# Three orders changed in a one-core encoder layer: mixing's first splits, the opening of cross-attention, the end of the down projection

## The chip, the cores and the metric

The kernel runs on one core of one Trainium2 chip. The time is the device time of one execution in microseconds (us); lower is better. The core has five engines, each with an instruction queue of its own that is worked off in order: TensorE (PE: matmuls and transposes), VectorE (DVE), ScalarE (ACT), GpSimd (POOL) and SyncE (SP), which here issues nearly all DMAs. An instruction waits on semaphores until what it reads is written and what it overwrites has been read; everything behind it on its engine waits with it.

## The reference

One step of an encoder layer for 2048 prompt rows (16 tiles of 128) and 128 sample rows (one tile, 8 streams of 16), width 1024:

```python
def encoder_layer(x, ...):
    h = rmsnorm(x, g_mix_pre)
    y, new_k, new_v, new_conv = parallel_mixer(h, ...)   # band attention (8 heads) | depthwise conv, then @ w_out
    x = x + rmsnorm(y, g_mix_post)
    h = rmsnorm(x, g_mem_pre)
    x = x + rmsnorm(memory_attention(h, mk, mv, w_mq, w_mo), g_mem_post)   # 4 heads, 256 memory rows
    h = rmsnorm(x, g_ffn_pre)
    f = (silu(h @ w_gate) * (h @ w_up)) @ w_down                           # hidden width 2816
    return x + rmsnorm(f, g_ffn_post)
```

## The kernel before

Every large matmul is made in three: both operands are split into a high and a low part (`hi` in a rounded format, a cast on ScalarE; `lo = x - hi`, mostly on VectorE), and the products hi·hi, hi·lo and lo·hi are summed in PSUM (`mm3`, `mm3h`). So each operand tile costs one cast and one subtraction before TensorE can use it, and "split" below means these two.

The phases follow each other: memory projections; input projection and convolution; band attention; mixing (`mixout`); cross-attention (`cross_open` begins it, `phase_cross` goes on); gate and up projections (`gate_up`); `down`. A scheduling layer orders the instructions of each engine at build time by its own estimates and priorities. `issue_after(ins)` forces every instruction written inside it that runs on the engine of `ins` to stand behind `ins` there; instructions on other engines, DMAs among them, are not held. In the traces `sbf`, `sbr` and `sbx` are the large SBUF regions (plain numbers; split halves), `flexb` further SBUF pieces, `psb` PSUM.

Three places matter:

1. *Attention to mixing.* `attention()` walks over 128 units (head, tile): scores, softmax (`L802` reduces on VectorE, `L804` takes exponentials on ScalarE), transposes of the probabilities (`L883`, split by `L884` and `L885`), products with the values (`L896`, of which `L900` and `L902` gather the result). One sample stream goes along with each head; at its end two copies on VectorE (`L852`, `L853`) take its result from a PSUM buffer. `weigh` turns the softmax sums of one tile into factors: its transpose (`L970`) uses the same ring of three PSUM buffers. Meanwhile the output weights are loaded and split (`wload`: `L277`, `L278`); four of the eight remain for `mixout`. There `prep(t)` splits a tile's convolution half and its attention half (`L1024`, `L1025`), and the products with the output weights (`L291`) begin with the sample tile, then tile 0.
2. *Mixing to cross-attention.* `cross_open` is called inside the last mixed tile. It loads and splits the first cross weights `f1` (0 and 1 of 8) and norms tile 0: `prenorm` squares (`L308`), scales (`L315`), transposes (`L318`), casts the high half (`L319`) and subtracts the low one (`L320`). `phase_cross` loads `f1` 2 to 7 and the value weights `f2` (`L1218`, split in `L1221` and `L1222`; the subtractions of `f1` 1, 3 and 5 are on GpSimd) through three staging buffers `stg`. `scores` of tile 0 are 48 products, in whose midst `second()` norms tile 1; the scores of tile 1 follow, with `probs` of tile 0 (`L1280` to `L1284`) in between. The postnorm of the sample's cross-attention (`L339` to `L341`) and of the last mixed tiles (`L1071` to `L1077`) run at the same time.
3. *The end of `down`.* Seven weight forms are gone through in the order 0, 1, 3, 4, 5, 6, 2; each has three groups of tile pairs, a group three PSUM products of 11 blocks. The activation block is loaded (`L1596`) and split (`L1601`, `L1602`) once for the group's products. `evict` adds a product into `ys`; a tile that is complete is normed and stored by `finish` (`L351` squares, `L352` multiplies by the gain, `L300` and `L301` take the power, `L357` scales and adds the residual, loaded at `L1613` into one of two buffers). Form 2 completes tiles 12, 13 and the sample tile last; there `finish` works in two halves.

Of the kernel before, what the change touches and what calls it, by code (L numbers as in the profile page):

```python
# [8 lines left out]
F32 = mybir.dt.float32  # L9
# [3 lines left out]
ALU = mybir.AluOpType  # L13
# [4 lines left out]
P = 128  # L18
D = 1024
# [19 lines left out]
F2 = 2  # L39
SLAST = NPT * (H - 1) + 4  # L40
# [96 lines left out]
class Build:  # L137
# [173 lines left out]
    def prenorm(self, pool, pspool, xt, gbc, hi, lo, tag="tr", keep=False):  # L311
        nc = self.nc
        r = self.rms(pool, xt[:, :])
        h = self.t(pool, [P, D], F32, "hn", 1) if keep else xt
        nc.vector.scalar_tensor_tensor(h[:, :], xt[:, :], r[:, :], gbc[:, :], ALU.mult, ALU.mult)  # L315
        ps = self.t(pspool, [P, KC, P], F32, tag)
        for k in range(KC):
            self.last_transpose = nc.tensor.transpose(ps[:, k, :], h[:, k * P:(k + 1) * P], self.ident[:, :])  # L318
        nc.scalar.copy(hi, ps[:, :, :])  # L319
        nc.vector.tensor_tensor(lo, ps[:, :, :], hi.bitcast(F32), ALU.subtract)  # L320
# [22 lines left out]
    def finish(self, pool, y, xt, gbc, dst, parts, engine):  # L343
# [5 lines left out]
        yg = self.t(pool, [P, D], F32, "po")  # L349
# [442 lines left out]
    def attention(self):  # L792
# [14 lines left out]
        def sample(s):  # L807
# [45 lines left out]
            nc.vector.tensor_copy(self.attS[DH:, :, ss], po[DH:, :, DEC_S:])  # L853
# [135 lines left out]
    def mixout(self, ctx):  # L989
# [13 lines left out]
        for _ in self.wo_load:  # L1003
            pass
# [33 lines left out]
        with self.tc.high_priority(offset=HP2):  # L1038
            for t in order[:2]:
                prep(t)  # L1040
# [202 lines left out]
    def phase_cross(self, ctx):  # L1243
# [79 lines left out]
        todo = [(g, p) for g in range(3) for p in range(3)]  # L1323
        def second():
            hq[1] = norm(1)
# [5 lines left out]
        with self.tc.issue_after(self.last_mo.ins):  # L1331
# [181 lines left out]
    def down(self, ctx):  # L1513
# [12 lines left out]
                .at("y", 4, *[(a, [0]) for a in fy]))  # L1526
# [60 lines left out]
        for i, j in enumerate(order):  # L1587
            w = nxt
            nxt = []
            for g in range(3):  # L1590
                np_ = 3 if g < 2 or j in (0, 2, 4, 6) else 2
                ps = [self.t(ps_mm, [P, 512], F32, "mm") for _ in range(np_)]
                for f0 in range(0, NF // 2, 2):
# [3 lines left out]
                    for x in range(nf):  # L1597
# [5 lines left out]
                        fp = f0 + x  # L1603
                        for p in range(np_):
# [5 lines left out]
                for p in range(np_):  # L1610
                    for t in evict(j, g, p, ps[p]):
                        xt = self.t(pool, [P, D], F32, "xt")
                        nc.sync.dma_start(xt[:, :], self.x2[t])  # L1613
                        end = i == len(order) - 1 and g == 2
                        self.finish(pool, ys[t], xt, gpost, self.rows("y", t), 2 if end else 1,
                                    nc.vector if end else nc.gpsimd)
# [74 lines left out]
```

## Time and profile before

| | |
|---|---|
| time, median of 3 runs | 2942.23 us (2939.48 to 2942.48) |
| profiled execution | 2946.83 us, its span 2945.0 us |
| mean granted TensorE clock | 0.994 |
| DMA | 500.04 MB in 198154 packets, mean 170 GB/s |
| chain that ended last | PE 41%, DMA 4%, POOL 3%, DVE 2% of the span |

The span is counted from the first to the last instruction of the program on the chip. Rows of a timeline give start and length in us, engine, line, operation, what is written from what, sizes, a count of like instructions, and in brackets the idle time of the engine before it and what ended it. A "window" row gives, for a stretch of the span, the busy time of each engine with its count of instructions, the clock that TensorE was granted (1.00 is full), the share of the DMA engines and GB/s.

### The profile page before, as it was taken

What the parts mean: (1) busy time and instruction counts of PE and PEld (TensorE: products, weight loads), DVE (VectorE), ACT (ScalarE), POOL (GpSimd) and SP (SyncE); (2) the same over time, 40 slices, a digit from 0 to 9 for tenths busy, and PEclk for the clock granted to TensorE, in tenths of its full rate; (3) what the DMA queues carried; (4) which work ended last, traced back from release to release, by engine and by line L of the source; (5) the groups of instructions that cost most, each with busy time, mean ns of one, the idle gap of its engine ahead of it and who ended that gap; (6) DMA issues with size and microseconds to landing.
All of it is one profiled execution on the core that took longest, in us unless ns stands there. A gap on an engine that the chain in (4) does not pass through costs nothing.

```text
span 2945.0 us, 45369 instructions
## 1 busy us (share of the span) xinstructions
PE 2871.7 (98%) x16740; PEld 2623.9 (89%) x16740; DVE 2083.8 (71%) x3024; ACT 1308.8 (44%) x2661; POOL 1375.9 (47%) x1252
## 2 busy tenths in 40 slices
PE   8999999989999999999989999999999999999998
PEld 8999999979978777888879999999999999888786
DVE  6697795979985345344569788788788997556655
ACT  4535364669973234232344333433344444332433
POOL 0268396730023224144557565465556775424413
PEclk9999999999999999999999999999999999999999
DMA  8635255558845665133355333644344446756754
GB/s 306 248 115 174 97 162 172 161 173 202 214 141 193 214 228 179 57 127 102 129 196 176 115 133 115 201 161 156 135 148 143 149 141 224 224 172 227 226 192 163
DMA packets 198154, 500.04 MB, mean 170 GB/s; under 512 B 18981, under 2 KB 87085, under 8 KB 189603
## 3 DMA queue, kind: packets, MB, share of 16 engines
q1 hardware_dynamic: 187211, 459.78, 48.3%
q0 software_dynamic: 10720, 37.36, 3.3%
q8 instruction: 131, 2.15, 0.3%
q14 instruction: 92, 0.75, 0.1%
HBM read 365.97 MB, written 141.81 MB: 172 GB/s over the span
## 4 chain that ended last, share of the span: by engine, by line
PE 41%; DMA 4%; POOL 3%; DVE 2%; issue 1%; ACT 0%; DVEq 0%; SPq 0%; POOLq 0%; ACTq 0%
PE psb L285 13%; PE psb L283 13%; PE psb L284 13%; PE psb L291 1%; DMA sbf<-x 1%; DMA sbf<-in_w_down_dram 1%; POOL sbf L1541 1%; DMA sbf<-hn 1%; PE psb L1396 1%; DMA sbf<-in_w_gate_dram 0%; DVE sbr L1419 0%; POOL sbf L340 0%; DMA out_dram<-sbf 0%; DVE sbr L1602 0%; DMA hn<-sbf 0%
## 5 line engine op out<-in xcount | busy, mean ns | idle before, releaser
L283 PE MATMUL psb<-sbr 128*128 128x384 f32 (+3 forms) x2808 | 942.3, 337 | 4.4 <-ACT sbr L1601 1.9
L284 PE MATMUL psb<-sbr 128*128 128x384 f32 (+3 forms) x2356 | 805.3, 342 | 2.4 <-DVE sbr L320 2.4
L285 PE MATMUL psb<-sbr 128*128 128x512 f32 (+3 forms) x1848 | 633.1, 344 | 3.3 <-DVE sbr L1602 3.1
L283 PEld LDWEIGHTS psb<-sbr 128*128 128x128 f32 x2808 | 530.0, 189 | 34.4 <-ACT sbr L1601 3.4
L285 PE MATMUL psb<-sbr,sbx 128*128 128x384 f32 (+2 forms) x1484 | 476.4, 322 | 0.0
L284 PEld LDWEIGHTS psb<-sbr 128*128 128x128 f32 x2356 | 444.7, 189 | 29.4 <-DVE sbr L320 2.7
L285 PEld LDWEIGHTS psb<-sbr 128*128 128x128 f32 x1848 | 347.9, 189 | 33.3 <-DVE sbr L1602 6.6
L1419 DVE TENSOR_TENSOR sbr<-sbf,sbr 128x512 fp32r<-128x512 f32 x258 | 263.7, 1025 | 38.7 <-ACT sbr L1418 37.9
L1418 ACT CAST sbr<-sbf 128x512 fp32r<-128x512 f32 x258 | 159.4, 620 | 279.7 <-PE psb L284 223.6
L285 PEld LDWEIGHTS psb<-sbr,sbx 128*128 128x128 f32 x1484 | 280.3, 189 | 0.2
L523 DVE SCALAR_TENSOR_TENSOR psb<-sbf,psb 128x768 f32<-128x768 f32 (+1 forms) x290 | 264.3, 911 | 6.2
L291 PE MATMUL psb<-sbr 128*128 128x512 f32 x1004 | 247.3, 395 | 0.1
L1602 DVE TENSOR_TENSOR sbr<-sbf,sbr 128x384 fp32r<-128x384 f32 (+1 forms) x231 | 171.1, 763 | 94.6 <-ACT sbr L1601 93.7
L291 PEld LDWEIGHTS psb<-sbr 128*128 128x128 f32 x1004 | 185.9, 188 | 41.5 <-issue 2.5
L278 POOL TENSOR_TENSOR sbx<-sbf,sbr 128x1024 fp32r<-128x1024 f32 x60 | 153.1, 2553 | 81.6 <-ACT sbr L277 78.2
L1541 POOL TENSOR_TENSOR sbf<-sbf 128x512 f32<-128x512 f32 x77 | 107.5, 1401 | 169.7 <-DMA sbf<-in_w_down_dram 167.9
L1601 ACT CAST sbr<-sbf 128x384 fp32r<-128x384 f32 (+1 forms) x231 | 111.2, 497 | 166.5 <-PE psb L284 141.1
L533 POOL TENSOR_TENSOR flexb<-flexb,flexb 128x128 f32<-128x128 f32 (+1 forms) x180 | 167.5, 931 | 21.4 <-ACT flexb L532 12.0
L283 PE MATMUL psb<-sbr,sbx 128*128 128x384 f32 (+1 forms) x524 | 170.5, 327 | 2.2 <-ACT sbx L1418 1.5
L1418 ACT CAST sbx<-sbf 128x512 fp32r<-128x512 f32 x153 | 94.6, 620 | 162.2 <-PE psb L284 150.7
L291 PE MATMUL psb<-sbr,sbx 128*128 128x512 f32 x654 | 160.9, 397 | 3.7 <-ACT sbx L319 2.2
L1419 DVE TENSOR_TENSOR sbx<-sbf,sbx 128x512 fp32r<-128x512 f32 x153 | 152.3, 997 | 16.3 <-ACT sbx L1418 16.0
(333 smaller groups left out, 5938.4 us busy)
## 6 DMA issues: line engine op xcount, KB each, us to landing
af<-flexb SPq DMA_DIRECT2D x33, 1344.0 KB, 6.2
sbf<-in_w_down_dram SPq DMA_DIRECT2D x154, 256.0 KB, 3.7
sbf<-af SPq DMA_DIRECT2D x90, 384.0 KB, 4.0
sbf<-in_w_gate_dram SPq DMA_DIRECT2D x66, 512.0 KB, 3.4
sbf<-in_w_up_dram SPq DMA_DIRECT2D x66, 512.0 KB, 3.4
sbf<-x SPq DMA_DIRECT2D x50, 512.0 KB, 3.8
sbf<-in_w_in_dram SPq DMA_DIRECT2D x48, 512.0 KB, 3.7
sbr<-ks SPq DMA_DIRECT2D x28, 512.0 KB, 9.0
```

What stands on the lines that cost most here:

```text
L278: self.lo_engine.tensor_tensor(lo[:, :], wf[:, :], hi[:, :].bitcast(F32), ALU.subtract)
L283: nc.tensor.matmul(ps, lh, rh, start=start, stop=False, **kw)
L284: nc.tensor.matmul(ps, lh, rl, start=False, stop=False, **kw)
L285: self.last_product = nc.tensor.matmul(ps, ll, rh, start=False, stop=stop, **kw)
L291: self.last_half = nc.tensor.matmul(y[o], l, r[:, o * 512:(o + 1) * 512], start=start and x == 0, stop=stop and x == 2)
L523: nc.vector.scalar_tensor_tensor(acc if w < CW - 1 else o, src(w), cwt[:, j, w:w + 1], acc, ALU.mult, ALU.add)
L533: nc.gpsimd.tensor_tensor(o, o, v, ALU.add)
L1418: nc.scalar.copy(hs[j][:, :], src[j])
L1419: nc.vector.tensor_tensor(ls[j][:, :], src[j], hs[j][:, :].bitcast(F32), ALU.subtract)
L1541: nc.gpsimd.tensor_tensor(acc[:, :], acc[:, :], q[:, :], ALU.add if s > 0 else ALU.subtract)
L1601: nc.scalar.copy(ch[:, m], a[:, x, m])
L1602: nc.vector.tensor_tensor(cl[:, m], a[:, x, m], ch[:, m].bitcast(F32), ALU.subtract)
```

## The change

- In `sample`, the last copy is kept as `last_copy`. The output weights that `mixout` still has to split, and the splits of mixing's first two tiles, are put behind it on VectorE.
- `prenorm` keeps its cast and its subtraction (`last_hi`, `last_lo`). The loads of `f1` 2 to 7 and of the first two `f2`, and the norm of tile 1, are put behind those of tile 0's norm, on ScalarE and on VectorE.
- In the last group of `down`, the blocks 6 to 10 are split as before, but their products are made afterwards, tile by tile: 15 matmuls for tile 12, then its eviction and norm, then tile 13, then the sample tile. The three residuals get buffers of their own, loaded at the group's start in the program, and the gain products too.

```diff
+LATE = 5
@@ prenorm
-        nc.scalar.copy(hi, ps[:, :, :])
-        nc.vector.tensor_tensor(lo, ps[:, :, :], hi.bitcast(F32), ALU.subtract)
+        self.last_hi = nc.scalar.copy(hi, ps[:, :, :])
+        self.last_lo = nc.vector.tensor_tensor(lo, ps[:, :, :], hi.bitcast(F32), ALU.subtract)
@@ finish
-        yg = self.t(pool, [P, D], F32, "po")
+        yg = self.t(pool, [P, D], F32, tag)
@@ sample
-            nc.vector.tensor_copy(self.attS[DH:, :, ss], po[DH:, :, DEC_S:])
+            self.last_copy = nc.vector.tensor_copy(self.attS[DH:, :, ss], po[DH:, :, DEC_S:])
@@ mixout
-        for _ in self.wo_load:
-            pass
+        with self.tc.issue_after(self.last_copy.ins):
+            for _ in self.wo_load:
+                pass
...
-        with self.tc.high_priority(offset=HP2):
+        with self.tc.high_priority(offset=HP2), self.tc.issue_after(self.last_copy.ins):
             for t in order[:2]:
                 prep(t)
@@ phase_cross
+        def behind():
+            stack = ExitStack()
+            stack.enter_context(self.tc.issue_after(self.last_hi.ins))
+            stack.enter_context(self.tc.issue_after(self.last_lo.ins))
+            return stack
+
         def second():
-            hq[1] = norm(1)
+            with behind():
+                hq[1] = norm(1)
...
-        with self.tc.issue_after(self.last_mo.ins):
+        with self.tc.issue_after(self.last_mo.ins), behind():
             f1 += [f1_load(k) for k in range(2, KC)]
             f2 = [load(self.f2s[:, k, :], f"f2{k}") for k in range(F2)]
@@ down
+                end = i == len(order) - 1 and g == 2
+                if end:
+                    xe = []
+                    for t in (12, 13, S_TILE):
+                        xe.append(self.t(pool, [P, D], F32, "xe"))
+                        nc.sync.dma_start(xe[-1][:, :], self.x2[t])
+                late = []
...
+                        if end and fp >= NF // 2 - LATE:
+                            late.append((ch, cl, fp))
+                            continue
...
                 for p in range(np_):
+                    for ch, cl, fp in late:
+                        c = slice(p * P, (p + 1) * P)
+                        self.mm3(ps[p][:, :], ch[:, c], cl[:, c], w[fp][0][:, :], w[fp][1][:, :],
+                                 False, fp == NF // 2 - 1)
                     for t in evict(j, g, p, ps[p]):
-                        xt = self.t(pool, [P, D], F32, "xt")
-                        nc.sync.dma_start(xt[:, :], self.x2[t])
-                        end = i == len(order) - 1 and g == 2
+                        if end:
+                            xt = xe[p]
+                        else:
+                            xt = self.t(pool, [P, D], F32, "xt")
+                            nc.sync.dma_start(xt[:, :], self.x2[t])
```

Line numbers of the changed program are higher by one (`L319` becomes `L320`) to some 17 (`down`). Place 1, VectorE at the end of the last head, before (`ISA` is a softmax reduction and its read-out, the two `COPY` are the sample's):

```order
L885 TENSOR_TENSOR sbr<-psb,sbr 128x512 x2
L1025 TENSOR_TENSOR sbr<-flexb_153,sbr 128x512
L278 TENSOR_TENSOR sbr<-sbf,sbr 128x1024
L802 ISA flexb_157<-psb,flexb_153 128x640
L802 ISA flexb_157 128x1
L802 ISA flexb_153,flexb_157<-psb,flexb_153 128x640
L802 ISA flexb_157 128x1
L852 COPY sbf<-psb 64x4x16
L853 COPY sbf<-psb 64x4x16
```

and now:

```order
L886 TENSOR_TENSOR sbr<-psb,sbr 128x512 x2
L803 ISA flexb_157<-psb,flexb_153 128x640
L803 ISA flexb_157 128x1
L803 ISA flexb_153,flexb_157<-psb,flexb_153 128x640
L803 ISA flexb_157 128x1
L853 COPY sbf<-psb 64x4x16
L854 COPY sbf<-psb 64x4x16
L1027 TENSOR_TENSOR sbr<-flexb_153,sbr 128x512
L279 TENSOR_TENSOR sbr<-sbf,sbr 128x1024
```

The two splits moved behind the copies. TensorE at the same place, before (`ident` marks transposes) and now:

```order
L896 MATMUL psb<-sbx,sbr 128x128 x2
L970 MATMUL psb<-ident_73,sbr 16x128
L883 MATMUL psb<-ident_73,flexb_153 128x128 x4
L970 MATMUL psb<-ident_73,sbr 16x128
L291 MATMUL psb<-sbr 128x512 x4
L883 MATMUL psb<-ident_73,flexb_153 128x128 x4
L896 MATMUL psb<-sbr 128x128 x2
```

```order
L897 MATMUL psb<-sbx,sbr 128x128 x2
L971 MATMUL psb<-ident_73,sbr 16x128
L292 MATMUL psb<-sbr 128x512 x4
L884 MATMUL psb<-ident_73,flexb_153 128x128 x8
L971 MATMUL psb<-ident_73,sbr 16x128
L897 MATMUL psb<-sbr 128x128 x2
```

Mixing's first four matmuls now stand ahead of the transposes of probabilities.

Place 2, VectorE at the opening of cross-attention, before and now (`sbx<-psb,sbx` and the last `sbr<-psb,sbr` are the low halves of the first and second norm, `sbr<-sbf,sbr` weights, 128x512 x2 a mixed tile's scaling):

```order
L315 SCALAR_TENSOR_TENSOR sbf<-sbf 128x1024
L1222 TENSOR_TENSOR sbr<-sbf,sbr 128x1024
L339 SCALAR_TENSOR_TENSOR flexb_153<-psb,flexb_153 128x1024
L1222 TENSOR_TENSOR sbr<-sbf,sbr 128x1024
L315 SCALAR_TENSOR_TENSOR sbf<-sbf 128x1024
L320 TENSOR_TENSOR sbx<-psb,sbx 128x1024
L1222 TENSOR_TENSOR sbr<-sbf,sbr 128x1024 x3
L1075 SCALAR_TENSOR_TENSOR flexb_153<-psb,flexb_153,sbf 128x512 x2
L315 SCALAR_TENSOR_TENSOR sbf<-sbf 128x1024
L320 TENSOR_TENSOR sbr<-psb,sbr 128x1024
```

```order
L316 SCALAR_TENSOR_TENSOR sbf<-sbf 128x1024
L340 SCALAR_TENSOR_TENSOR flexb_153<-psb,flexb_153 128x1024
L1077 SCALAR_TENSOR_TENSOR flexb_153<-psb,flexb_153,sbf 128x512 x2
L321 TENSOR_TENSOR sbx<-psb,sbx 128x1024
L1224 TENSOR_TENSOR sbr<-sbf,sbr 128x1024 x2
L316 SCALAR_TENSOR_TENSOR sbf<-sbf 128x1024
L1224 TENSOR_TENSOR sbr<-sbf,sbr 128x1024 x2
L316 SCALAR_TENSOR_TENSOR sbf<-sbf 128x1024
L1077 SCALAR_TENSOR_TENSOR flexb_153<-psb,flexb_153,sbf 128x512 x2
L321 TENSOR_TENSOR sbr<-psb,sbr 128x1024
```

All weights from the third on moved behind the first norm's low half; on ScalarE the casts moved likewise behind its high half. GpSimd there, before and now (the 128x1 operations are powers of the norms, `sbr<-sbf,sbr` the subtractions of `f1` 3 and 5):

```order
L1222 TENSOR_TENSOR sbr<-sbf,sbr 128x1024
L340 TENSOR_TENSOR flexb_153<-flexb_153,sbf 128x1024
L1222 TENSOR_TENSOR sbr<-sbf,sbr 128x1024
L341 DMA x_16_70_142<-flexb_153 128x1024
L1072 TENSOR_TENSOR flexb_153<-flexb_153 128x1
L300 TENSOR_SCALAR flexb_153<-flexb_153 128x1
L301 TENSOR_TENSOR flexb_153<-flexb_153,mhalf_78 128x1
L1076 TENSOR_TENSOR flexb_153<-flexb_153 128x1024
```

```order
L341 TENSOR_TENSOR flexb_153<-flexb_153,sbf 128x1024
L342 DMA x_16_70_142<-flexb_153 128x1024
L1078 TENSOR_TENSOR flexb_153<-flexb_153 128x1024
L1224 TENSOR_TENSOR sbr<-sbf,sbr 128x1024
L1079 DMA x_14_51_123<-flexb_153 128x1024
L301 TENSOR_SCALAR sbf<-sbf 128x1
L1074 TENSOR_TENSOR flexb_153<-flexb_153 128x1
L302 TENSOR_TENSOR sbf<-sbf,mhalf_78 128x1
```

The subtraction of `f1` 3 moved behind two residual sums and a store.

Place 3, VectorE at the end of the program, before and now (`psb` is read by the evictions):

```order
L1579 TENSOR_TENSOR flexb_21126<-flexb_21126,psb 128x512
L1579 TENSOR_TENSOR flexb_21130<-flexb_21130,psb 128x512
L352 TENSOR_TENSOR sbf<-flexb_21126,sbf 128x512
L1559 TENSOR_TENSOR flexb_21134<-flexb_21134,psb 128x512
L352 TENSOR_TENSOR sbf<-flexb_21130,sbf 128x512
L357 SCALAR_TENSOR_TENSOR sbf<-sbf 128x512 x4
L352 TENSOR_TENSOR sbf<-flexb_21134,sbf 128x512 x2
L357 SCALAR_TENSOR_TENSOR sbf<-sbf 128x512 x2
```

```order
L1589 TENSOR_TENSOR flexb_21126<-flexb_21126,psb 128x512
L353 TENSOR_TENSOR flexb_21150<-flexb_21126,sbf 128x512
L358 SCALAR_TENSOR_TENSOR flexb_21138<-flexb_21150,sbf,flexb_21138 128x512 x2
L1589 TENSOR_TENSOR flexb_21130<-flexb_21130,psb 128x512
L353 TENSOR_TENSOR flexb_21154<-flexb_21130,sbf 128x512
L1569 TENSOR_TENSOR flexb_21134<-flexb_21134,psb 128x512
L358 SCALAR_TENSOR_TENSOR flexb_21142<-flexb_21154,sbf,flexb_21142 128x512 x2
L353 TENSOR_TENSOR flexb_21158<-flexb_21134,sbf 128x512
L358 SCALAR_TENSOR_TENSOR flexb_21146<-flexb_21158,sbf,flexb_21146 128x512 x2
```

Each tile's chain now stands behind its own eviction; on SP the three residual loads moved from between the last stores into the last group of form 5.

More of the change, by code (lines that the diff above doesn't have):

```diff
@@ L341, in postnorm, with finish @@
         nc.gpsimd.dma_start(dst, o[:, :])
-    def finish(self, pool, y, xt, gbc, dst, parts, engine):
+    def finish(self, pool, y, xt, gbc, dst, parts, engine, tag="po"):
         nc = self.nc
@@ L1525, in down @@
                 .at("ch", 1.5, (sbR, [68, 71, 74, 77, 48, 51])).at("cl", 1.5, (sbR, [69.5, 72.5, 75.5, 78.5, 49.5, 52.5]))
-                .at("y", 4, *[(a, [0]) for a in fy]))
+                .at("y", 4, *[(a, [0]) for a in fy])
+                .at("xe", 4, *[(a, [0]) for a in fy[9:12]]).at("pe", 4, *[(a, [0]) for a in fy[12:15]]))
         ps_mm = Region().at("mm", 2, (self.ps, [12, 14, 8, 10, 0, 2, 4, 6]))
@@ L1610, in down @@
                 for p in range(np_):
+                    for ch, cl, fp in late:
+                        c = slice(p * P, (p + 1) * P)
+                        self.mm3(ps[p][:, :], ch[:, c], cl[:, c], w[fp][0][:, :], w[fp][1][:, :],
+                                 False, fp == NF // 2 - 1)
                     for t in evict(j, g, p, ps[p]):
-                        xt = self.t(pool, [P, D], F32, "xt")
-                        nc.sync.dma_start(xt[:, :], self.x2[t])
-                        end = i == len(order) - 1 and g == 2
+                        if end:
[3 more added lines that the diff above has]
+                            nc.sync.dma_start(xt[:, :], self.x2[t])
                         self.finish(pool, ys[t], xt, gpost, self.rows("y", t), 2 if end else 1,
-                                    nc.vector if end else nc.gpsimd)
+                                    nc.vector if end else nc.gpsimd, "pe" if end else "po")
 _ORDER = ["mem", "proj", "att", "cross", "ffn"]
```

## The prediction

> **What bounds the kernel.** I read the page first, then TensorE's waits, then the last microseconds of the chain, then each engine's timeline at the three places of the change. The page's head, and the long waits of TensorE (the columns are what waited, on what, us in total, times, longest; the last row is of the down stage alone):
>
> ```profile
> span 2945.0 us, 45369 instructions
> ...
> PE 2871.7 (98%) x16740; PEld 2623.9 (89%) x16740; DVE 2083.8 (71%) x3024; ACT 1308.8 (44%) x2661; POOL 1375.9 (47%) x1252
> PE psb L970 <- DVE sbf L853: 3.8, 1, 3.8
> PE psb L291 <- ACT sbx L319: 2.2, 1, 2.2
> PE psb L291 <- DVE sbx L320: 1.4, 1, 1.4
> PE psb L318 <- DVE sbr L1284: 0.9, 1, 0.9
> PE psb L285 <- DVE sbr L1602: 2.4, 2, 1.7
> ```
>
> TensorE is the bound, busy 98%. Only its holes and the tail behind it can be won, and the matmuls are the same before and after. The first four waits lie at the change's first two places.
>
> **Place 1, end of the last head.** VectorE, TensorE and ScalarE (start, length), then windows (length, busy time of PE, PEld, DVE, ACT, POOL, granted clock, DMA share, GB/s):
>
> ```profile
> 858.08 2.90 DVE L1025 TENSOR_TENSOR sbr<-flexb,sbr 128x512 fp32r<-128x512 f32 x1 [0.17 <-PE psb L866]
> 860.90 1.21 DVE L278 TENSOR_TENSOR sbr<-sbf,sbr 128x1024 fp32r<-128x1024 f32 x1
> 863.75 0.23 DVE L853 COPY sbf<-psb 64x64 f32<-64x64 f32 x1
> 858.78 1.48 PE L896 MATMUL psb<-sbx,sbr 128*128 128x512 f32 x8
> 864.03 0.28 PE L970 MATMUL psb<-ident,sbr 128*16 128x128 f32 x1 [3.77 <-DVE sbf L853]
> 868.04 2.74 PE L896 MATMUL psb<-sbr 128*128 128x128 f32 x16
> 858.88 1.04 ACT L884 CAST sbr<-psb 128x512 fp32r<-128x512 f32 x2
> 860.35 0.58 ACT L900 COPY flexb<-psb 64x512 f32<-64x512 f32 x1 [0.43 <-PE psb L896]
> 863.72 0.81 ACT L804 ACTIVATE flexb<-flexb,flexb 128x640 f32<-128x640 f32 x1
> 864.53 0.60 ACT L1024 CAST sbr<-sbf 128x512 fp32r<-128x512 f32 x1
> 864.00:868.00 4.00, 3.52 (x13) 2.77 (x14) 3.80 (x11) 2.12 (x6) 0.00 (x0) 0.57 0.61 225
> 868.00:892.00 24.00, 23.93 (x141) 20.53 (x140) 12.41 (x19) 11.70 (x19) 1.86 (x2) 1.00 0.34 113
> ```
>
> TensorE's transposition at L970 needs a buffer that the last sample's copies (L852, L853) still read. They stand on VectorE behind two splits that nobody needs yet: the convolution half of mixing's first tile (2.90 us) and an output weight (1.21). TensorE stops for 3.77 us, and then has a clock of 0.57 for 4 us, 4.0 x 0.43 = 1.7 us lost. From 868 on it is full again: what is won ahead of 868.04 stays won, unless something later comes late.
>
> **Place 2, opening of cross-attention.** TensorE, ScalarE, VectorE, GpSimd, SP, a window, and the landing times of the eight loads of cross weights:
>
> ```profile
> 1123.37 1.52 PE L291 MATMUL psb<-sbr 128*128 128x512 f32 x6
> 1127.13 2.06 PE L291 MATMUL psb<-sbr,sbx 128*128 128x512 f32 x4 [2.25 <-ACT sbx L319]
> 1135.52 1.03 PE L318 MATMUL psb<-ident,sbf 128*128 128x128 f32 x8
> 1136.31 7.06 PE L291 MATMUL psb<-sbr,sbx 128*128 128x512 f32 x30
> 1143.21 8.55 PE L291 MATMUL psb<-sbr 128*128 128x512 f32 x37
> 1157.78 0.70 PE L291 MATMUL psb<-sbr 128*128 128x512 f32 x2
> 1126.08 1.01 ACT L319 CAST sbx<-psb 128x1024 fp32r<-128x1024 f32 x1
> 1133.68 1.22 DVE L1222 TENSOR_TENSOR sbr<-sbf,sbr 128x1024 fp32r<-128x1024 f32 x1 [0.88 <-ACT sbr L1221]
> 1122.67 2.40 POOL L1222 TENSOR_TENSOR sbr<-sbf,sbr 128x1024 fp32r<-128x1024 f32 x1
> 1125.02 3.35 POOL L340 TENSOR_TENSOR flexb<-flexb,sbf 128x1024 f32<-128x1024 f32 x1
> 1131.62 0.63 POOL L341 DMA_DIRECT2D x<-flexb  x1
> 1125.10 0.32 SPq L1218 DMA_DIRECT2D sbf<-f1s  x1
> 1127.10:1130.60 3.50, 2.06 (x4) 1.14 (x4) 3.48 (x2) 0.10 (x1) 3.50 (x2) 0.51 0.64 252
> DMA to landing us min/median/max: 4.7/7.2/10.6
> ```
>
> The first norm's high half (L319) starts at 1126.08, though its transposes stand ahead of the matmuls at 1123.37: ScalarE casts cross weights first. Its low half (L320) waits on VectorE likewise. Full speed by these rows: (1143.21 - 1136.31) / 30 = 0.23 us a matmul, (1136.31 - 1135.52) / 8 = 0.1 a transposition. From the last mixing matmul (six from 1123.37, so 1124.7) to the start at 1157.78 TensorE has 48 + 48 matmuls of two tiles' scores, 4 of values and 24 transpositions: 23.0 + 2.4 us, free at 1150.1. So 7.7 us are lost here in waits and slow clock.
>
> **Place 3, the tail.** TensorE's last matmul, and pieces of the chain behind it (start, length):
>
> ```profile
> 2930.61 0.39 PE L285 MATMUL psb<-sbr 128*128 128x512 f32 x1
> 2929.68 0.70 DVE flexb L1579
> 2930.46 0.73 ACT sbf L351 x2
> 2932.06 0.55 POOL sbf L301
> 2936.49 3.67 DMA sbf<-x
> 2940.27 0.06 DVE sbf L357
> ```
>
> TensorE is done at 2931.0, the span ends at 2945.0: 14 us in which three tiles are normed one behind the other, and the last one's scaling (L357) waits until 2940.27 for its residual, a load that stands on SP behind the four stores of the other two.
>
> **The sum, part by part.**
>
> *Tail.* The last five products of tile 12, then 13, then the sample tile are made in one block each, 15 matmuls; the residuals are loaded a stage ahead, and each product has a buffer of its own. By 0.23 x 15 = 3.4 us a block, tile 12 is complete 6.8 us and tile 13 3.4 us ahead of the end. Only the sample tile's chain is left: eviction at 2931.0, ScalarE 0.78 later (2930.46 - 2929.68), GpSimd's power done 2.93 after the eviction's start (2932.06 + 0.55 - 2929.68), so the scaling starts at 2934.0 instead of 2940.27. The two scalings, their stores and what follows stay as they are. **6.3 us**; if VectorE still finishes tile 13's pair first, a microsecond less, 5.3; if the chain of the lone tile is shorter for having GpSimd to itself, 7 at most. The cover is gone only if the fifth split comes late: the block of tile 12 eats a split every 0.7 us instead of 2.0, from 2920.8. The splits wait for buffers that the first six products free, so all stand ready by about 2921.
>
> *First splits behind the copy.* The two score reductions and the copies take 1.9 us (860.90 + 1.21 to 863.75 + 0.23), so from 858.08 they are done at 860.0, when TensorE ends L896 (858.78 + 1.48): the wait of 3.77 goes. What is late next: four mixing matmuls now stand directly behind the transposition, and need the cast at L1024. ScalarE reaches it after two casts (858.88 + 1.04), two exponentials of 0.81 and the copy of 0.58, at 862.1, and ends 0.60 later: from 860.5 TensorE waits 2.2 us. Then 4 x 0.23 + 9 x 0.1 = 1.8 us of work: L896 at 864.5 at full clock, 866.2 with the 1.7 us of slow clock, instead of 868.04. Place 2 shows that 2.25 us of waiting is enough for the clock to fall (0.51 behind it), so I take 1.8, less 0.3 for the splits that now follow the weight's cast on ScalarE: **1.5 us**, between 0 (the same wait again) and 5.7 (3.77 + 1.7, and the rest of this gap). On SP a load for the sample's query and one of cached keys go ahead of convolution tiles; these come up to 1 us later, onto a ScalarE that is then busy with the weight.
>
> The Trainium skill speaks against my slow clock: its page "TensorE: Matmul & The Clock Gate", section "What's actually happening", lets the clock fall only after an idle window of about 3.4 us. This trace has it at 0.51 behind 2.25 us of idleness, so I go by the trace; by the page the sum would be 12.0 us instead of 9.5.
>
> *Cross weights and second norm behind the first norm.* Now L319 follows its transposes, which stand twelve matmuls ahead of the scores; its 1.01 and a low half like the other splits' 1.22 are there before the fifth score matmul at 1125.7, and both waits, 2.25 and 1.4, go. What is late next are the weights. Three staging buffers feed eight loads; a load waits until both engines have split what was there. In the row of SP the seventh weight is issued at 1125.10, when GpSimd has split the fourth (1122.67 + 2.40); the last weight is split at 1134.90, 9.8 us later. After the change the fourth's split stands on GpSimd behind the sample's residual (L340, 3.35), its store (0.63) and tile 14's residual, another 2.4 to 3.35. L340 itself starts earlier than 1125.02, at the latest at 1122.6 without the 2.40 of the fourth's split ahead of it, and as the second and third norm's small operations now follow too, at about 1120.5 (an estimate): the fourth is done at 1120.5 + 3.35 + 0.63 + 2.4 + 2.4 = 1129.3, by the slower values at 1131.2. Plus 9.8, less 0.4 since the last load then no longer waits for its own buffer: the last weight at 1138.7. Behind it VectorE has the third norm, tile 15's scaling and only then the second norm's low half, three operations of a tile's width at the last split's 1.22, 3.7 us; then 44 + 4 matmuls and 16 transpositions, 12.6: 1155.0 instead of 1157.8, 2.8 us. TensorE waits near 2 us once for that low half; half of a 1.7 us clock loss off: **2.0 us**. Bounds: 7.7 if nothing waits; with the longest landing for the shortest (10.6 - 4.7 = 5.9) and a full clock loss, 2.8 - 5.9 - 1.7 = -4.8. The second norm's own start costs nothing: its transposes stand 32 score matmuls behind, 7.4 us that hide it; without that cover it would be one more wait of VectorE's 1.22 and ScalarE's 1.01.
>
> *Loads moved.* The three residuals, 1.5 MB, now move two stages earlier (BFORM 5 instead of 2), where SP holds them until GpSimd has read the sums whose place they take, with activation loads queued behind. TensorE already waits there for splits of activations at L1602 (2.4 us in all). **-0.3**, between 0 and that wait once more, -2.4. The buffers and the changed names cost nothing.
>
> Sum: 6.3 + 1.5 + 2.0 - 0.3 = 9.5 us. The profiled execution took 2946.83 (span 2945.0, 1.8 around it), so 2937.3 for one like it; the median of the runs is 2942.23, so **2932.7 us**.
>
> **Rivals.**
> - A wait takes the place of each wait at places 1 and 2, and only the tail is won: 2942.2 - 6.0 = 2936.2. For it: at both places something else is due within 2 us.
> - All waits go, at both places: 2942.2 - 5.7 - 7.7 - 6.3 = 2922.5. Against it: ScalarE's order at place 1.
> - The waits shorten as I say, but the clock holds: 1.7 + 0.8 more, 2930.2. Against it the 0.51. The Trainium skill's page cited above would have this for the new waits, all below its window.
> - The tail doesn't do what it says: a split or a store still holds tile 13, and 2 us of its gain go: 2934.7, with places 1 and 2 at nothing 2938.2.
> - Slower: the last three cross weights load one behind the other, each at 10.6 us, from 1126: the last split at 1160, 16.3 more to the values, 18.6 us lost against 1157.8, so 2942.2 - 7.5 + 18.6 = 2953.3. It decides from a last weight later than 1149. Against it: before, two of them were in flight together.
>
> **How the numbers follow.** Forecast 0.46, tail alone 0.22, all waits 0.10, clock holds 0.08, weak tail 0.10, serial loads 0.04. The forecast's own range is 2928.5 to 2936. From 2926 to 2938.5 only all waits, serial loads and a little of the forecast's and the weak tail's edges stay out, under 0.2. About 0.2%, 5.9 us, is what a measurement of this kernel can tell; so faster means under 2936.3: the forecast, all waits, clock holds and half of tail alone, 0.75. Slower has serial loads, 0.04. The rest, 0.21, is the same.
>
> **What would show it.** Right: about 7.7 us between TensorE's last matmul and the end; no wait on L853's successor, but one near 2.2 us on the cast of the attention half; the second tile's scores waiting near 2 us on a VectorE split, the values' matmuls starting at most 3 us sooner. Wrong: the tail's last store still behind a load; the scores waiting for weights beyond 1149; a clock of 1.00 behind both waits.

## The result, and the profile after

The changed kernel takes 2937.95 us (median of 22 runs, 2934.34 to 2940.66), the kernel before on the same chip 2942.86 (22 runs). The ratio on record is 0.9976, with a 95% interval of 0.9970 to 0.9982; by it the change saves 7.1 us (the two medians alone lie 4.9 apart). Its profiled execution took 2939.08 us, with a span of 2937.3 against 2945.0, 7.7 less. The runs of one kernel differ by 6 to 12 us among themselves, and profiles too: code that is the same in all is up to 5 us longer or shorter from one profile to the next (from the values' first matmul to the program's last 1771.5 us in this profile, 1767.0 and 1772.0 in e_sqrt and e_po below). So what a place is worth is read at the place.

Lines of the changed kernel are one higher than before up to mixing, two higher there and at the opening of cross-attention, eight to ten higher from there to gate and up, 10 to 26 higher in `down` (`L853` is `L854`, `L1222` is `L1224`, `L1602` is `L1619`). The page's head, and then TensorE's waits that answer to those of before:

```profile
span 2937.3 us, 45362 instructions
...
PE 2872.8 (98%) x16740; PEld 2625.5 (89%) x16740; DVE 2081.9 (71%) x3024; ACT 1308.1 (45%) x2661; POOL 1370.5 (47%) x1252
```

```profile
PE psb L292 <- POOL sbr L1224: 3.3, 2, 2.7
...
PE psb L292 <- ACT sbr L1026: 1.6, 1, 1.6
...
PE psb L971 <- DVE sbf L854: 0.6, 1, 0.6
PE psb L292 <- DVE sbx L321: 0.5, 1, 0.5
```

The wait of 3.8 us on the copy is now 0.6, with one of 1.6 on the cast of the attention half behind it. At place 2 the waits of 2.2 and 1.4 are gone; in their stead stand 3.3 on GpSimd and 0.5 on the first norm's low half.

Place 1, the timeline of the changed kernel (start, length), and a window (busy PE, PEld, DVE, ACT, POOL, clock, DMA share, GB/s):

```profile
857.65 1.47 PE L897 MATMUL psb<-sbx,sbr 128*128 128x512 f32 x8
859.72 0.28 PE L971 MATMUL psb<-ident,sbr 128*16 128x128 f32 x1 [0.60 <-DVE sbf L854]
861.62 1.19 PE L292 MATMUL psb<-sbr 128*128 128x512 f32 x4 [1.62 <-ACT sbr L1026]
864.15 3.75 PE L897 MATMUL psb<-sbr 128*128 128x128 f32 x16
```

```profile
862.00:866.00 4.00, 4.00 (x20) 3.75 (x19) 3.87 (x11) 1.32 (x3) 0.00 (x0) 0.61 0.65 205
```

The eight matmuls at 857.65 are 1.13 us earlier than before (858.78); that is scatter, since with the same order they begin at 859.95 in e_po. The sixteen matmuls begin 3.89 earlier (868.04 then), but 3.75 us long instead of 2.74: the slow clock, 0.61 over four microseconds, now falls on them.

Place 2:

```profile
1120.36 1.52 PE L292 MATMUL psb<-sbr 128*128 128x512 f32 x6
1121.72 1.07 PE L292 MATMUL psb<-sbr,sbx 128*128 128x512 f32 x4
1123.32 4.09 PE L292 MATMUL psb<-sbr,sbx 128*128 128x512 f32 x16 [0.53 <-DVE sbx L321]
1127.99 3.15 PE L292 MATMUL psb<-sbr,sbx 128*128 128x512 f32 x12 [0.58 <-POOL sbr L1224]
1135.02 5.78 PE L292 MATMUL psb<-sbr,sbx 128*128 128x512 f32 x16 [2.69 <-POOL sbr L1224]
1154.99 0.71 PE L292 MATMUL psb<-sbr 128*128 128x512 f32 x2
1120.73 1.41 DVE L1077 SCALAR_TENSOR_TENSOR flexb<-psb,flexb,sbf 128x512 f32<-128x512 f32 x2 [5.88 <-DMA x<-flexb]
1122.06 1.21 DVE L321 TENSOR_TENSOR sbx<-psb,sbx 128x1024 fp32r<-128x1024 f32 x1
1128.54 0.53 POOL L301 TENSOR_SCALAR sbf<-sbf 128x1 f32<-128x1 f32 x1
1132.62 2.35 POOL L1224 TENSOR_TENSOR sbr<-sbf,sbr 128x1024 fp32r<-128x1024 f32 x1
```

From the last six mixing matmuls to the values' first (1120.36 to 1154.99) it takes 34.63 us; before, 34.41 (1123.37 to 1157.78). The early scores wait 0.53 and 0.58 us where 2.25 and 1.4 stood, and then TensorE stands 2.69 us for the sixth weight. Its split on GpSimd is behind the small operations of two norms and a postnorm, from 1128.54 on. And one row that I had not looked for: on VectorE tile 14's scaling (`L1077`) now stands ahead of the first norm's low half (`L321`), and waits for a store (5.88 us). The order at place 2, printed under "The change", already has it there.

The tail: TensorE's last matmul and the last scaling of the changed kernel, then what each engine's queue does at the very end (operation, count, shortest/median/longest in ns, first and last start), and the same of before:

```profile
2926.45 0.39 PE L286 MATMUL psb<-sbr 128*128 128x512 f32 x1
2929.62 0.55 POOL L302 TENSOR_TENSOR sbf<-sbf,mhalf 128x1 f32<-128x1 f32 x1
2930.20 1.41 DVE L358 SCALAR_TENSOR_TENSOR flexb<-flexb,sbf,flexb 128x512 f32<-128x512 f32 x2 [0.72 <-POOL sbf L302]
```

```profile
L1713 POOLq DRAIN  x3: 44/93/6895, 2929.6 to 2937.0; - x3
L1713 SPq DRAIN  x3: 7/7/7, 2934.1 to 2936.7; - x3
```

```profile
L1687 POOLq DRAIN  x3: 40/102/7284, 2935.5 to 2944.8; - x3
L1687 SPq DRAIN  x3: 7/7/7, 2944.2 to 2944.5; - x3
```

The scaling starts 3.4 us behind the last matmul's end (2926.83), near the 3.0 of the forecast, and SP, whose stores have landed by then, closes from 2934.1 on. But GpSimd closes with a drain of 6895 ns that begins at 2929.6: 2936.5. The closing semaphores of TensorE, ScalarE and VectorE start behind it, at 2936.7, and the span ends at 2937.3, 10.45 us behind the last matmul. Before, the same drain ended at 2942.7, ahead of SP's 2944.2, and did not show.

The 7.7 us of the profile by these rows: 1.1 ahead of place 1 (unchanged code); 1.9 at place 1 (857.65 to 1120.36, less the same of before); -0.2 at place 2; 1.4 between 1154.99 and the last matmul (unchanged code but for the loads); 3.5 behind it (14.39 to 10.85, from that matmul's start). So 2.5 of the 7.7 come from stretches that the change does not touch, but for the loads.

### The profile page after: what moved, and what is told of

It reads as the page before. It is cut to its first block, busy times and chain, and to the rows that moved or that the text cites. A ratio compares the mean times of both kernels' runs of the same rounds, so it can differ in the third digit from the quotient of the medians.

```text
span 2937.3 us, 45362 instructions
## 1 busy us (share of the span) xinstructions
PE 2872.8 (98%) x16740; PEld 2625.5 (89%) x16740; DVE 2081.9 (71%) x3024; ACT 1308.1 (45%) x2661; POOL 1370.5 (47%) x1252
## 4 chain that ended last, share of the span: by engine, by line
PE 42%; DMA 3%; DVE 3%; POOL 2%; issue 1%; ACT 0%; SPq 0%; DVEq 0%; POOLq 0%; ACTq 0%
PE psb L286 13%; PE psb L284 13%; PE psb L285 13%; DMA sbf<-in_w_down_dram 1%; PE psb L292 1%; POOL sbf L1551 1%; PE psb L1405 1%; DMA sbf<-x 1%; DMA sbf<-hn 1%; DVE sbr L1619 0%; DVE sbr L1428 0%; DMA sbf<-in_w_gate_dram 0%; DVE sbx L1428 0%; POOL sbf L341 0%; DMA hn<-sbf 0%
## 5 line engine op out<-in xcount | busy, mean ns | idle before, releaser
L1619 DVE TENSOR_TENSOR sbr<-sbf,sbr 128x384 fp32r<-128x384 f32 (+1 forms) x231 | 169.2, 756 | 93.1 <-ACT sbr L1618 91.4
L1618 ACT CAST sbr<-sbf 128x384 fp32r<-128x384 f32 (+1 forms) x231 | 111.0, 497 | 165.1 <-PE psb L285 142.8
```

What stands on the lines that cost most here:

```text
L1618: nc.scalar.copy(ch[:, m], a[:, x, m])
L1619: nc.vector.tensor_tensor(cl[:, m], a[:, x, m], ch[:, m].bitcast(F32), ALU.subtract)
```

## The experiments

All are timed against the kernel before. "The stretch" is that of place 2, from the last six mixing matmuls to the values' first.

### The tail

**e_tail.** Only the end of `down` is changed; places 1 and 2 as before.

> The end of the down stage alone; places 1 and 2 are as before. Theory A (read from the trace of the changed kernel): TensorE's last matmul to the end of the span takes 10.4 us instead of 14.0, so 3.6 us are won, not 6.3, because GpSimd closes the program 6.3 us after its last operation, which is now later than the last store; some 1 us more can come from loads of the down stage that stand otherwise. Expected 3.6 to 5 us faster than before. Rival B (the prediction's term): the tail gives 6.3 us, and the rest of the change gives little; expected 6.3 faster, with about 7.7 us between the last matmul and the end.

Ratio 0.9983 (0.9975 to 0.9992), 5.0 us faster; that interval, 2.4 to 7.4 us, holds A's and B's number alike. The profile decides: 10.45 us behind the last matmul, again with GpSimd's drain last (over at 2936.5). A holds: the tail itself gives 3.6 us, not 6.3.

**e_late0.** The blocks taken back, the early residuals kept.

```diff
-LATE = 5
+LATE = 0
```

> The changed kernel, with the last five products not held back: the residuals of the three last tiles are still loaded early into buffers of their own, but tile 12, 13 and the sample tile are complete within 0.7 us of each other. Theory A (most of the tail's gain is the blocks): three tiles are normed one behind the other, the last scaling starts near 6.5 us behind the last matmul instead of 3.2; the end comes about 13 us behind it instead of 10.45, 2.5 to 3 us slower than the changed kernel. Rival B (the gain is the residual that no longer waits): about 10.5 us, no difference.

13.14 us behind the last matmul, and the last scaling 6.07 us behind it instead of 3.37: the blocks are worth 2.7 us, as A said. The ratio, 0.9986 (0.9976 to 0.9995), is 2.9 us behind the changed kernel's, though the intervals overlap.

**e_noxe.** The blocks kept, the early loads of the residuals taken back.

```diff
-                if end:
-                    xe = []
...
-                        if end:
-                            xt = xe[p]
-                        else:
-                            xt = self.t(pool, [P, D], F32, "xt")
-                            nc.sync.dma_start(xt[:, :], self.x2[t])
+                        xt = self.t(pool, [P, D], F32, "xt")
+                        nc.sync.dma_start(xt[:, :], self.x2[t])
```

> The changed kernel, with the blocks of the last five products kept and the early loads of the residuals taken back: each of the three last tiles loads its residual when it is evicted, on SP behind the stores of the tile before. Theory A (the blocks alone carry the tail, as the run without them lost 2.7 us): 10.5 to 11.5 us from the last matmul to the end. Rival B (the sample tile's residual stands behind tile 13's stores again and lands 3.7 us after its issue, which gives back what the blocks win): 13 to 14 us, 2.5 to 3.5 us slower than the changed kernel.

```profile
2928.50 1.42 DVE L358 SCALAR_TENSOR_TENSOR sbf<-flexb,sbf 128x512 f32<-128x512 f32 x2 [2.55 <-DMA sbf<-x]
```

```profile
L1705 POOLq DRAIN  x3: 40/102/6897, 2926.0 to 2933.5; - x3
L1705 SPq DRAIN  x3: 7/7/7, 2932.4 to 2933.2; - x3
```

A is right in the number; of what B said, the wait is there, but not its cost. The scaling waits 2.55 us for its residual, and starts 5.20 us behind the last matmul (its end is at 2923.30). The end is still 10.45 behind it, since GpSimd's drain (over at 2932.9) hides SP's 2932.4. So the early loads, as the change stands, win nothing at the end. The ratio is 0.9983 (0.9974 to 0.9993), its interval overlapping that of the changed kernel.

**e_sqrt.** The last tile's inverse root off GpSimd.

```diff
-            nc.gpsimd.tensor_tensor(ss[:, 0:1], ss[:, 0:1], ss[:, x:x + 1], ALU.add)
-        r = self.rstd(pool, ss[:, 0:1], 1.0 / D)
+            small.tensor_tensor(ss[:, 0:1], ss[:, 0:1], ss[:, x:x + 1], ALU.add)
+        r = self.rstd(pool, ss[:, 0:1], 1.0 / D, small)
...
+            small.tensor_scalar(r[:, :], ss, scale, EPS, ALU.mult, ALU.add)
...
+            nc.scalar.activation(r[:, :], r[:, :], AF.Sqrt)
+            small.reciprocal(r[:, :], r[:, :])
```

> The changed kernel, with the last tile's sum, mean and inverse root taken from GpSimd: the sum and mean on VectorE, a square root on ScalarE, a reciprocal on VectorE. GpSimd's last operation is then tile 13's. Theory A (GpSimd's closing sets the end, 6.3 us after its last operation in all six profiles so far): GpSimd is through at about 3.1 us sooner than in the changed kernel, the end is set by SP's last store, and TensorE's last matmul to the end takes near 8.2 us instead of 10.45; 2 us faster than the changed kernel. Rival B (the end follows the last scaling by a fixed time, as the prediction had it): the scaling starts at about the same time, since ScalarE has to load a table for the root, so no difference, 10.4 us.

The closing of GpSimd and SP, and the end of the chain:

```profile
L1720 POOLq DRAIN  x3: 44/93/6895, 2926.9 to 2935.1; - x3
L1720 SPq DRAIN  x3: 7/7/7, 2934.6 to 2934.9; - x3
```

```profile
2928.86 1.28 ACT L306 ACT_TABLE_LOAD   x1
2930.66 1.41 DVE L364 SCALAR_TENSOR_TENSOR flexb<-flexb,sbf,flexb 128x512 f32<-128x512 f32 x2
```

The scaling starts 3.38 us behind the last matmul, as with GpSimd (VectorE is busy until 2930.19, which covers the table's 1.28 us). But GpSimd is through at 2933.8, SP at 2934.6 sets the end, and it takes 8.13 us instead of 10.45. That is the drain taken away with nothing else: 2.3 us, A. In the times, 0.9972 (0.9963 to 0.9981), it is not apart from the changed kernel's interval.

### Place 1

**e_place1.** Only the first splits behind the last copy; the rest as before.

> The first splits behind the last sample's copy, alone; place 2 and the tail as before. Theory A: the wait of 3.77 us on the copy becomes one near 0.6 on the copy and one near 1.6 on the cast of the attention half; the sixteen matmuls behind start 2.8 us sooner, and after the slow clock 1.9 us are left. Expected 1.9 us faster. Rival B (the prediction's term): 1.5 us. Rival C: nothing of it reaches the end, since later loads and splits hold their old times; 0.

Ratio 0.9986 (0.9977 to 0.9995), 4.1 us faster. The waits are those of the changed kernel to 0.02 us, the clock is not:

```profile
860.12 0.28 PE L971 MATMUL psb<-ident,sbr 128*16 128x128 f32 x1 [0.58 <-DVE sbf L854]
862.00 1.20 PE L292 MATMUL psb<-sbr 128*128 128x512 f32 x4 [1.61 <-ACT sbr L1026]
864.09 2.75 PE L897 MATMUL psb<-sbr 128*128 128x128 f32 x16
```

```profile
862.00:866.00 4.00, 4.00 (x24) 3.41 (x25) 3.87 (x11) 1.44 (x4) 0.00 (x0) 1.00 0.69 239
```

With the clock at 1.00 the place gives 3.3 us (in matmuls: from the 5780th to the 6000th it takes 41.99 us instead of 45.29). Of the eleven profiles here with this order the clock held in five, and this piece took 41.97 to 41.99; it fell in six, and it took 43.16 to 43.43. So the place is worth 3.3 or 2.0 us. The time, 1.5 to 6.8 us faster by its interval, shuts out C and does not tell A's 1.9 from B's 1.5.

Which of the two it is can be read from the clock's record. In every profile the clock stands at 0.50 or 1.00 and changes only in whole steps of 3.41 us; in that of the changed kernel it is 1.00 from 859.51 to 862.92, 0.50 until 866.33, and 1.00 again (0.61 is the mean over a window that cuts these steps). Where the steps begin differs from profile to profile. In the six where the clock fell here, TensorE had been busy for 0.36 to 0.50 of the step ahead of the fall (1.58 of 3.41 us in this profile); in the five where it held, its emptiest step here was busy for 0.55 to 0.65. So in these eleven profiles it is where the steps cut the gap that tells a fall from a hold. The busy share is not the whole rule: at place 2 the clock held behind steps of 0.45 to 0.50.

The Trainium skill's page "TensorE: Matmul & The Clock Gate", section "What's actually happening", has the clock judged over a window of 3.4 us that runs on freely, whatever the kernel does, so that the same work meets it at another phase each time. The record agrees, and that explains two clocks for one set of waits. That an idle window is needed does not fit: between 859 and 862 TensorE was busy for 0.78 us in the changed kernel, where the clock fell, and for 0.81 in e_place1, with no 3.4 us of idleness in either.

### Place 2

**e_place2** has only this part of the change, **e_no2** all but this part (the diff is that of e_no2 against the changed kernel):

```diff
-            with behind():
-                hq[1] = norm(1)
+            hq[1] = norm(1)
-        with self.tc.issue_after(self.last_mo.ins), behind():
+        with self.tc.issue_after(self.last_mo.ins):
```

> Cross weights and second norm behind the first norm's split, alone; place 1 and the tail as before. Theory A: the waits of 2.25 and 1.45 us become three of 0.5, 0.6 and 2.7 on the same first norm and on GpSimd's splits of the fourth and sixth weights, and the values' matmuls start within 0.3 us of where they did: no difference, 0 +- 1 us. Rival B (the prediction's term): 2.0 us faster, with a wait near 2 us on VectorE's split of the second norm's low half.

> The changed kernel with place 2 undone (cross weights and second norm as before). Theory A: the same as the changed kernel within 1 us, about 7 us faster than before (ratio 0.9976). Rival B: 2.0 us slower than the changed kernel, 5 us faster than before (ratio 0.9983).

e_place2: 1.0004 (0.9994 to 1.0013). e_no2: 0.9971 (0.9961 to 0.9981), 8.5 us faster than before, where the whole change gives 7.1. The waits in e_place2:

```profile
1127.43 4.08 PE L292 MATMUL psb<-sbr,sbx 128*128 128x512 f32 x16 [2.47 <-DVE sbx L321]
1138.87 5.80 PE L292 MATMUL psb<-sbr,sbx 128*128 128x512 f32 x16 [2.42 <-POOL sbr L1223]
1124.83 1.41 DVE L1076 SCALAR_TENSOR_TENSOR flexb<-psb,flexb,sbf 128x512 f32<-128x512 f32 x2 [5.87 <-DMA x<-flexb]
1126.16 1.21 DVE L321 TENSOR_TENSOR sbx<-psb,sbx 128x1024 fp32r<-128x1024 f32 x1
```

The wait on the low half is there too, 2.47 us, and its cause: tile 14's scaling overwrites the buffer from which the sample's sum is being stored, and VectorE stands before it for 5.87 us with the low half behind. In all five profiles with the whole of place 2 and nothing else there, the scaling starts 3.1 us behind the issue of that store. In that of the changed kernel the store was issued 2.74 us ahead of the last six mixing matmuls, and the wait was 0.53; in e_noxe, e_place2, e_late0 and e_sqrt it was issued 1.18, 0.80, 0.52 and 0.34 us ahead of them, and the wait was 2.09, 2.47, 2.76 and 2.95. Over all profiles with one of the two orders, the stretch took, in us:

| order of place 2 | kernels | stretch | mean |
|---|---|---|---|
| old | before, e_tail, e_place1, e_no2, e_best | 34.41, 32.91, 33.93, 33.91, 33.53 | 33.74 |
| new | changed, e_place2, e_sqrt, e_late0, e_noxe | 34.63, 35.82, 36.01, 37.35, 36.15 | 35.99 |

Place 2 does not give 2 us, it takes 2.25 at the values. A had nothing here, from the one profile that was the best of five; B had a gain; at the values both fell. The times (1.2 us slower alone, 1.5 faster without it) point the same way. They shut out B, whose ratios, 0.9993 and 0.9983, lie just outside the intervals, but not A's nothing.

**e_second.** The weights as before, only the second norm behind (`behind()` kept around `norm(1)`, taken from the loads).

> The changed kernel, with the cross weights as before and only the second norm kept behind the first norm's split. Theory A (the second norm's scaling, 3.4 us on VectorE, made the first norm's low half late; the weights moved behind it made the rest late): the wait on the cast stays at 2.0 to 2.4 us, the wait of 1.5 to 2 us on the low half goes or falls under 0.5, and no wait on GpSimd appears: 32 to 33 us from the last six mixing matmuls to the values' first, against 33.9 with the old order and 34.6 with the new. Rival B: the low half is then late for another reason (tile 14's scaling, which waits for a store), and the stretch stays at 34 us.

Ratio 0.9990 (0.9981 to 1.0000). The wait on the cast stayed, at 1.69, and the one on the low half went, as A said. But the stretch is 39.0 us (1121.15 to 1160.16), against A's 32 to 33 and B's 34: a value weight's cast, which waits 4.28 us for its load, now stands on ScalarE ahead of the probabilities' cast, and TensorE waits 5.42 us for the latter (`L1285`).

**e_dve.** The change, with two more subtractions on VectorE.

```diff
-                        nc.gpsimd if k in (1, 3, 5) else nc.vector)
+                        nc.gpsimd if k == 1 else nc.vector)
```

> The changed kernel, with the low halves of the fourth and sixth cross weight on VectorE instead of GpSimd. Theory A (at place 2 GpSimd's queue, with the sample's and tile 14's residuals and eight small operations, makes the weights late): the wait of 2.7 us on GpSimd's split of the sixth weight goes, a smaller one on VectorE or on a load takes its place, and the values' matmuls come 1 to 2 us nearer to the first norm's: 33 to 34 us behind the last six mixing matmuls instead of 34.6. Rival B (the three staging buffers and the landing of the loads set it): the wait stays near 2.7 us, only on another engine, 34.6 us.

36.33 us (1121.15 to 1157.48), ratio 0.9986 (0.9977 to 0.9995). The wait on GpSimd is gone; 1.97 on the low half, 1.33 on a weight's cast and 2.22 on VectorE's split stand there. So GpSimd's queue alone is not the cause. That is B, though its 34.6 was too short as well.

**e_po.** The change, with the sample's sum in a buffer of its own.

```diff
-        self.postnorm(pool, flat(y), xt, gpost, self.x2[S_TILE], bufs=1)
+        self.postnorm(pool, flat(y), xt, gpost, self.x2[S_TILE], bufs=1, tag="sh")
```

In `postnorm`, `tag` becomes an argument that names the buffer.

> The changed kernel, with one edit: the sample's sum goes into a buffer of its own (that of its normed input, which is dead by then), so that tile 14's scaling on VectorE no longer waits for the sample's store to land. Theory A (place 2 loses because, in the new order, tile 14's scaling stands on VectorE ahead of the first norm's low half and waits there for that store; 36 us from the last six mixing matmuls to the values' first in three of four profiles with the new order, 33.8 in the mean of four with the old): the wait of 2.5 to 3 us on the low half of the first norm goes or falls to 0.5, the one near 2.7 on GpSimd stays or shrinks by less than 1, and the stretch takes 33.5 to 34.5 us; the kernel is 1.5 to 2.5 us faster than the changed kernel. Rival B (the low half is late for the cast, or the weights' ring sets the end whatever comes first): the stretch stays at 35 to 36 us, no difference in time.

The wait on the low half is gone altogether, as A had it. But 1.95 us on GpSimd's split and 3.87 on VectorE's of the last weight remain, and the stretch is 37.05 (1121.26 to 1158.31), nearer to B's 35 to 36 than to A's 33.5 to 34.5. Ratio 0.9985 (0.9975 to 0.9994).

**e_po_dve.** Both edits.

> As the run before, and the low halves of the fourth and sixth cross weight on VectorE. Theory A (with tile 14's scaling free, GpSimd's queue is the last thing that makes the weights late): the wait on the sixth weight falls from near 2.7 to under 1.5 us, and the stretch takes 32.5 to 33.5 us. Rival B (the loads' landing sets it: in the run with this edit alone a wait of 1.3 us on a cast and one of 2.2 on VectorE stood in its place): the stretch is that of the run before within 0.5 us.

```profile
1121.08 1.52 PE L292 MATMUL psb<-sbr 128*128 128x512 f32 x6
1122.44 6.97 PE L292 MATMUL psb<-sbr,sbx 128*128 128x512 f32 x30
1134.45 1.65 PE L292 MATMUL psb<-sbr,sbx 128*128 128x512 f32 x6 [1.67 <-DVE sbr L1224]
1152.73 0.71 PE L292 MATMUL psb<-sbr 128*128 128x512 f32 x2
1122.07 3.49 DVE L1224 TENSOR_TENSOR sbr<-sbf,sbr 128x1024 fp32r<-128x1024 f32 x3
```

31.65 us: thirty score matmuls in one run, three short waits (0.37, 1.67, 0.68), and the values 4.3 us sooner than in the mean of the new order, 2.1 sooner than in the old. A holds, with more than it said. Either edit alone gave nothing (36.33, 37.05 against 35.99), both give 4.3: two hindrances one behind the other, each able to hold the scores by itself. Each of these is one profile, and the new order alone spreads from 34.63 to 37.35; 31.65 lies 3.0 under its lowest. The first three splits took 3.49 us together; in the changed kernel two beside GpSimd's work took 5.84:

```profile
1123.19 5.84 DVE L1224 TENSOR_TENSOR sbr<-sbf,sbr 128x1024 fp32r<-128x1024 f32 x2
1124.59 3.35 POOL L1224 TENSOR_TENSOR sbr<-sbf,sbr 128x1024 fp32r<-128x1024 f32 x1
```

So the second edit does not only empty GpSimd's queue; for these three it also takes the two engines out of each other's way (a later one still took 3.42 us beside a residual sum on GpSimd). How the gain divides between these two was not tried. The ratio is 0.9972 (0.9960 to 0.9985, six runs), not apart from the changed kernel's.

### The best two parts

**e_best.** Place 2 undone, and the root off GpSimd.

> Place 2 undone, and the last tile's root off GpSimd: the two edits that gave most, together. If they are independent: 8.5 us (place 2 undone) and 1.4 to 2.3 more, 10 to 11 us faster than before, ratio 0.9963 to 0.9966, with 8.1 us from TensorE's last matmul to the end. If what the tail gives depends on the queue ahead of it: ratio 0.9971, as place 2 undone alone.

Ratio 0.9972 (0.9963 to 0.9981), where e_no2 has 0.9971. The tail took 8.14 us, as in e_sqrt, so the 2.3 us are there; but this profile was 1.7 us behind that of before at the 1000th matmul, 160 us in, and had the slow clock at place 1. (e_sqrt was 2.1 behind there, the others at most 0.6; the instructions are the same, and whether that is chance is open.) The intervals are 5 us wide, so whether the two parts add up in the time stays open. No version here is faster than the changed kernel by more than its interval. e_po_dve with the root off GpSimd, which by the rows should win 4.3 and 2.3 us on the change, was not tried.

## Why the prediction was right or wrong

The time lies in the range, 0.55 us from its slow end and outside the forecast's own 2928.5 to 2936; 2937.3 for an execution like the profiled one stood against 2939.08. The sum was 9.5 us, and 7.1 came. The terms were further off than that, and in both directions: at the three places the profiles show 3.6, 2.0 to 3.3 and -2.25 us, 3.4 to 4.7 in all. Where the rest of the 7.1 comes from stays open, so that the sum came this near is luck in part.

- *Tail, 6.3 forecast, 3.6 measured.* The scaling at 3.0 us behind the last matmul: 3.37. That the other tiles are out of the way by then: yes, 2.7 us without the blocks. SP's part came as forecast, its drain 7.3 us behind the last matmul instead of 13.2, 5.9 sooner. The failed step is "The two scalings, their stores and what follows stay as they are": what follows was GpSimd's drain, 1.5 us short of being the bound before (2942.7 against 2944.2), and it became the bound. The rival of a weak tail had about the size (2 us less), and another cause.
- *Place 1, 1.5 forecast.* The wait of 3.77 went but for 0.6, and the cast of the attention half came late, at 1.6 us instead of 2.2. What failed is the clock as one value: I let it fall for certain, and it falls in six of eleven profiles, by where its steps cut the gap. The place gives 2.0 us with that, 3.3 without; here the rival in which the clock holds is right in the other five.
- *Place 2, 2.0 forecast, -2.25 measured.* Right: the wait on the first norm's cast goes, and the weights come late, the fourth's split on GpSimd behind the residuals. Wrong first: "its 1.01 and a low half like the other splits' 1.22 are there before the fifth score matmul". I went through ScalarE's and GpSimd's queues and not through VectorE's, where tile 14's scaling had come to stand ahead and waits for a store. Wrong second: the wait near 2 us on the second norm's low half is not there, because the sixth weight, on GpSimd, holds TensorE 2.4 to 2.7 us before it gets that far. The forecast carried the old 9.8 us on from the fourth weight and had the last one at 1138.7; it was split at 1137.2, which is 1140.2 in the times of before (3.0 us of the shift were there by then), 1.5 later, and behind TensorE's wait of 2.69 the clock fell.
- *Loads moved, -0.3.* Within what can be told: from cross-attention to the end TensorE waits 3.5 us for the subtractions of activations (`L1619`) and 1.2 for their casts (`L1618`), before 3.1 and 1.9.
- *The rivals.* By the 7.1 us saved, the weak tail (7.5) and the tail alone (6.0) are nearest; the median, 2937.95, is nearest to the weak tail with the other places at nothing, 2938.2. None has the reasons: place 1 gave 2 to 3.3 us, place 2 took 2.25 back, and the tail gave 3.6. Serial loads: no, the last weight was split at 1137.

## What to carry to other kernels

Read how each engine closes the program, and not only the last store: here GpSimd's last operation stood 6.3 us ahead of the end of its closing, so of the 5.9 us by which the last store came sooner 3.6 counted, and the profile gave the rest once its last three small operations went elsewhere. When work is held behind an instruction, go through the queue of every engine that the held and the holding chain use, and ask of each instruction that comes to stand ahead whether it waits for a transfer. And where one hindrance is removed and nothing comes, remove the next as well before the place is given up: two edits that were worth nothing alone gave 4.3 us at the values together, in one profile each.

## What the runs showed of the hardware

- GpSimd's closing drain ended 6.30 or 6.31 us after the end of its last operation in all fourteen profiles, whether that operation took 0.55 or 0.94 us. What it does in that time no run shows.
- The clock fell or held behind the same waits, to 0.02 us, from run to run, by where its steps of 3.41 us cut them. In e_tail it held at place 2, over 4.4 us in which TensorE was busy for 1.24:

```profile
1124.60:1129.00 4.40, 1.24 (x5) 0.67 (x4) 4.38 (x2) 1.35 (x2) 4.40 (x2) 1.00 0.65 230
```

The two steps that cut this gap were busy for 1.95 and 1.67 of 3.41 us. Before, the clock had fallen to 0.51 behind a wait of 2.25, which left 0.34 of one step busy.

- VectorE's subtraction of 128x1024 took 1.22 us alone; the two beside GpSimd's operations of that size took 2.52 and 3.40. The Trainium skill's page "SBUF — State Buffer", section "SBUF: two separate sides", has GpSimd and a VectorE operation with two inputs in SBUF take turns at a shared pair of ports, each for a whole instruction. The rows of the changed kernel agree: the two engines' operations end in turn, GpSimd at 1124.62, VectorE at 1125.70, GpSimd at 1127.94, VectorE at 1129.02, each 1.1 or 2.2 us behind the other's, which is near what it takes alone (1.22 and 2.35).
